# Attention weights and values of the two dilated groups stacked by residue

## The chip, the cores and the metric

The kernel runs on one core of a Trainium2 chip. The metric is the device time of one execution in microseconds (us); lower is better. The kernel before was timed three times: 780.74 us median, 780.69 to 781.08. One further execution was taken with the hardware profiler; it took 780.72 us, and its profile spans 778.9 us, so 1.82 us lie outside the span.

## The reference, cut to what matters

The model is a trunk of two layers on 256 tokens of width 1024. The first layer mixes tokens with a short convolution, the second with dilated window attention; each layer also has a squared-ReLU MLP (4096 wide) and a gated per-layer input. The change is inside the attention of the second layer. It has 8 heads of 128 channels, and each head exists in three groups with their own queries, keys and values:

```python
DILATED_PATTERNS = ((128, 1), (512, 4), (2048, 16))   # (window, dilation) of groups 0, 1, 2
...
    for g, (window, dilation) in enumerate(DILATED_PATTERNS):
        o_g, lse_g = dilated_window_attention(q[:, :, g], k[:, :, g], v[:, :, g], window, dilation)
        outs.append(o_g)
        lses.append(lse_g)
    weights = jax.nn.softmax(jnp.stack(lses, axis=0), axis=0)
    o = jnp.sum(weights[..., None] * jnp.stack(outs, axis=0), axis=0)
```

In group 0 a query sees the keys of up to 128 tokens back. In group 1 it sees only keys whose distance is a multiple of 4, in group 2 only keys whose distance is a multiple of 16. The three results are weighted by the softmax of their log-sums, which is the same as one softmax over the scores of all three groups side by side, followed by one sum over all their values.

## The kernel before, in words

**Number format.** Most products are done with each float32 operand split into two parts in the format `fp32r`: `hi`, the rounded value, and `lo`, the rest. ScalarE (ACT) writes `hi`, VectorE (DVE) writes `lo` by subtraction, and TensorE (PE) adds the products hi·hi, hi·lo and lo·hi in PSUM. Weights come from memory in slabs of up to 8 blocks of 128x128 (`load_to`, L335), are split by ACT (L356) and DVE (L295, the helper `sub`) in `split_to`, and used in `block` (L392). Five raw slabs and six split slabs are buffered, and `weights` asks for the split of the slab five ahead (`LOOK`, L34).

**Order.** `make_plan` (L139) writes the whole program out as one list: products, and steps (`("do", name, ...)`) between them. The scheduler of the tile language keeps this order as priority on every engine, and each engine then works through its own queue in order.

**Token order.** From the attention on, tokens are sorted by residue (`residue_order`, L41): first by t mod 4, then by t mod 16, then by t div 16. So each half `b` of 128 tokens holds two residues mod 4 of 64 tokens each. A query of groups 1 and 2 only ever sees keys of its own run of 64 tokens, since a distance that is a multiple of 4 keeps the residue mod 4. The kernel before uses only that it stays within its half of 128.

**One head**, with the lines the prediction speaks of:

- `qk` products give queries and keys, two banks of PSUM per group. `add_up` calls `sums` (L411 ACT, L412 DVE), which adds the two partial sums and frees the banks. `qk_out` (L639) applies the rotary embedding on GpSimd (POOL: L644, L647, L653), for head 0 in part on DVE. `qk_split` (L656) splits group 0 into hi and lo (L429 ACT, L295 DVE).
- `v` products give the values of all three groups, one bank per half of the tokens, 384 columns. `v_out` (L659) takes them out, scaled by the norm of each token: group 0 as hi (L665 ACT) and lo (L666 DVE), groups 1 and 2 together as 256 columns (L667 ACT) into `v12`, in plain float32.
- `scores` (L671): per half, three products of 256 columns for group 0 (L677) and one float32 product of 128 columns for each of groups 1 and 2 (L680), all into one bank of 512 columns. Then the softmax over 512 columns: mask and maximum (L683 DVE), the negated maximum (L686 DVE), exponential and sum (L687 ACT), reciprocal (L688 DVE), scaling (L689 ACT) in place into `sm`.
- `turn` (L692): four transposes of 128x128 per half (L698 PE), two for group 0 and one for each of groups 1 and 2, into two banks. The first is split into hi and lo (L429 ACT, L295 DVE), the second copied by ACT (L703) into `pT12`, 512 columns.
- `values` (L706): six products for group 0 (L713), then for each half and each of groups 1 and 2 one float32 product of 128 columns (L719), all added up in one bank. L730 (ACT) and L731 (DVE) split the result into hi and lo for the output product `w_o`.

A float32 product appears in the trace as two passes of PE, each with its own weight load (LDWEIGHTS, listed as engine PEld); an `fp32r` product and a transpose appear as one.

**Overlap.** While the products of head h run, the plan puts between them `scores`, `turn` and `values` of head h-1 (L198 to L205). For head 0 these steps come one place later (`late`), `values` of head 0 even within head 2. The steps of the last head lie between the `w_o` products (L208 to L213).

Of the kernel before, what the change touches and what calls it, by code (L numbers as in the profile page):

```python
# [12 lines left out]
AF = mybir.ActivationFunctionType  # L13
ALU = mybir.AluOpType

P = 128
S = 256
# [5 lines left out]
GROUPS = 3  # L23
# [17 lines left out]
def residue_order(t):  # L41

    return (t % 4) * 64 + (t % 16 // 4) * 16 + t // 16
# [210 lines left out]
def tile_trunk(ctx: ExitStack, tc: tile.TileContext, plan, slabs, ap, out):  # L254
    nc = tc.nc
# [10 lines left out]
    def act(name, dtype=F32):  # L266
        return apool.tile([P, 2, S], dtype, tag="act", name=name)
# [20 lines left out]
    def f32(t):  # L288
        return t.bitcast(F32)

    def flat(t):
        return t.rearrange("p i s -> p (i s)")
# [20 lines left out]
    rstd, rows, cur, mask, by_token = {}, {}, {}, {}, {}  # L313
# [5 lines left out]
    offsets, n = [], 0  # L319
# [6 lines left out]
    for si, s in enumerate(slabs):  # L326
# [3 lines left out]
        at = 0  # L330
# [71 lines left out]
    def close(name):  # L402
        opened.discard(name)

        return acc.pop(name)
# [21 lines left out]
    def split_into(kind, j, src):  # L427
        hi, lo, t = pair(f"{kind}{j}", "pp" if kind in ("p0", "p1") else "pair")
        nc.scalar.activation(hi, src, AF.Copy)  # L429
        sub(lo, src, hi)  # L430
        state[kind][j] = (hi, lo, t)
# [226 lines left out]

    def v_out(head):  # L659

        v0, v12 = act(f"v0_{head}", F32R), act(f"v12_{head}")
        for b in (0, 1):
            p, r = flat(close(("v", b, head))), rstd[3][:, b : b + 1]
            hi, lo = v0[:, b, :P], v0[:, b, P:]
            nc.scalar.activation(hi, p[:, :P], AF.Copy, scale=r)  # L665
            nc.vector.scalar_tensor_tensor(lo, p[:, :P], r, f32(hi), ALU.mult, ALU.subtract)  # L666
            nc.scalar.activation(v12[:, b, :], p[:, P : GROUPS * P], AF.Copy, scale=r)  # L667
        cur["v", head] = v0, v12


    def scores(head):  # L671
        for b in (0, 1):
            own = slice(b * P, (b + 1) * P)
            ps = psum.tile([P, 512], F32, tag="ps", name=f"sc{head}_{b}")
            hi, lo, _ = state["qk"][head]
            for n, (q, k) in enumerate(((hi, hi), (hi, lo), (lo, hi))):
                nc.tensor.matmul(ps[:, :S], q[:, 0, own], k[:, 1, :], start=n == 0, stop=n == 2)  # L677
            for g in (1, 2):
                t = cur["qk", head, g]
                nc.tensor.matmul(ps[:, (g + 1) * P : (g + 2) * P], t[:, 0, own], t[:, 1, own], start=True, stop=True)  # L680
# [7 lines left out]
            nc.vector.reciprocal(stats[2], stats[2])  # L688
            nc.scalar.activation(sm, sm, AF.Copy, scale=stats[2])  # L689
            cur["pr", head, b] = sm  # L690

    def turn(head):  # L692

        ps = [bank(f"tp{head}_{n}") for n in (0, 1)]
        for b in (0, 1):
            sm = cur.pop(("pr", head, b))
            for n in range(4):
                nc.tensor.transpose(  # L698
                    ps[n // 2][:, n % 2, b * P : (b + 1) * P], sm[:, n * P : (n + 1) * P], ident
                )  # L700
        split_into("pT", head, ps[0])
        t = act(f"pT12_{head}")
        nc.scalar.activation(t, ps[1], AF.Copy)  # L703
        cur["pT12", head] = t

    def values(head):  # L706
        ps = bank(f"o{head}")
        v0, v12 = cur.pop(("v", head))
        hi, lo, _ = state["pT"].pop(head)
        for kb in (0, 1):  # L710
            vhi, vlo = v0[:, kb, :P], v0[:, kb, P:]
            for n, (a, b) in enumerate(((vhi, hi), (vhi, lo), (vlo, hi))):
                nc.tensor.matmul(  # L713
                    ps[:, 0, :], a, b[:, kb, :], start=kb == 0 and n == 0, stop=False, skip_group_check=True
                )
        t = cur.pop(("pT12", head))
        for b in (0, 1):
            for g in (0, 1):
                nc.tensor.matmul(  # L719
                    ps[:, 0, b * P : (b + 1) * P],  # L720
                    v12[:, b, g * P : (g + 1) * P],
                    t[:, g, b * P : (b + 1) * P],
                    start=False,
                    stop=g == 1,
                    skip_group_check=True,
                )
# [3 lines left out]
        nc.scalar.activation(hi, ps[:, 0, :], AF.Copy)  # L730
        nc.vector.tensor_tensor(lo, ps[:, 0, :], f32(hi), ALU.subtract)  # L731
# [116 lines left out]
def masks():  # L848

    import numpy as np  # L850

    t = np.argsort([residue_order(t) for t in range(S)])
    m = np.full((P, 2, 512), NEG, np.float32)
    for b in range(2):
        q = t[b * P : (b + 1) * P, None]
        for keys, to, window, step in (
            (t, slice(0, S), 128, 1),
            (t[b * P : (b + 1) * P], slice(S, S + P), 512, 4),
            (t[b * P : (b + 1) * P], slice(S + P, S + 2 * P), 2048, 16),
        ):  # L860
            d = q - keys[None]
            m[:, b, to][(d >= 0) & (d <= window) & (d % step == 0)] = 0.0
    return m


# [56 lines left out]
```

## Time and profile before

| What | Before |
|---|---|
| median of 3 runs | 780.74 us |
| profiled execution, its span | 780.72 us, 778.9 us |
| PE busy | 770.7 us (99% of the span), 4860 matmuls |
| DVE, ACT, POOL busy | 570.9, 440.7, 166.8 us |
| granted TensorE clock | 0.998 |
| one middle head (437.97 to 467.06 us) | 29.09 us; PE 29.09, DVE 21.37, ACT 17.38, POOL 21.43 us busy |

Times in a trace are counted from the start of the span. In the view of single instructions a row gives the start, the length, the engine, the line, the operation, the tiles it writes and reads, how many instructions are merged, and in brackets how long the engine sat idle before it and for whom. A merged row reaches from the start of its first instruction to the end of its last. PE's rows overlap, since a product starts while the one before still drains; what a product costs in a dense stream is therefore the distance to the next one, not its own length. The chain of waits shows this distance directly: it gives, piece by piece, the time by which the end moved on.

### The profile page before, as it was taken

Reading aid. Unit: us, or ns where it says so; the run is one execution under the profiler, and the core shown is the slowest. Engines: PE = TensorE matmul, PEld = TensorE weight load, DVE = VectorE, ACT = ScalarE, POOL = GpSimd, SP = SyncE. Lnnn points to the kernel's source line nnn. Section 1 sums busy time; section 2 is a strip of 40 time slices with the busy share of each in tenths; the row PEclk is TensorE's granted clock in tenths of the full one; section 3 lists DMA queues with packets and bytes.
Section 4 is the critical chain, followed back from the end, with each engine's and each line's share of the span. In section 5 each row is a group of like instructions: output and inputs, shape, how many; then the busy total and the mean of one; then the engine's idle time right before and its main releaser. Section 6 shows DMA issues by size and latency. Waiting matters only on the chain.

```text
span 778.9 us, 12519 instructions
## 1 busy us (share of the span) xinstructions
PE 770.7 (99%) x4860; PEld 702.2 (90%) x4860; DVE 570.9 (73%) x817; ACT 440.7 (57%) x679; POOL 166.8 (21%) x110
## 2 busy tenths in 40 slices
PE   9999999999999999999999999999999999999996
PEld 8999998888888899989989989989988888888885
DVE  6897779898556669788768768767698887555564
ACT  8654565565444447557655655655675555444454
POOL 0000000000000000177867867865000000000002
PEclk9999999999999999999999999999999999999999
DMA  9855555655555554655455455455456555565521
GB/s 325 289 192 190 187 188 178 194 184 195 186 192 186 191 181 158 202 179 156 157 175 163 149 176 163 151 173 190 136 196 185 188 191 189 187 191 189 188 94 55
DMA packets 42539, 140.97 MB, mean 181 GB/s; under 512 B 4848, under 2 KB 6128, under 8 KB 42480
## 3 DMA queue, kind: packets, MB, share of 16 engines
q1 hardware_dynamic: 41904, 139.52, 56.1%
q8 instruction: 38, 0.62, 0.3%
q10 hardware_dynamic: 576, 0.66, 0.3%
q14 instruction: 21, 0.17, 0.1%
HBM read 139.10 MB, written 1.05 MB: 180 GB/s over the span
## 4 chain that ended last, share of the span: by engine, by line
PE 97%; issue 1%; DMA 1%; DVE 0%; POOL 0%; SPq 0%; POOLq 0%; ACT 0%; DVEq 0%
PE acc_u L392 23%; PE acc_d L392 23%; PE acc_qk L392 17%; PE acc_v L392 9%; PE acc_o L392 6%; PE acc_g L392 5%; PE acc_C L392 3%; PE acc_B L392 3%; PE acc_X L392 3%; PE acc_p L392 1%; PE o L719 1%; PE sc L680 1%; PE tp L698 1%; PE sc L677 1%; PE o L713 1%
## 5 line engine op out<-in xcount | busy, mean ns | idle before, releaser
L295 DVE TENSOR_TENSOR wlo<-raw,whi 128x1024 fp32r<-128x1024 f32 (+2 forms) x277 | 350.7, 1272 | 162.5 <-ACT whi L356 160.4
L356 ACT ACTIVATE whi<-raw 128x1024 fp32r<-128x1024 f32 (+2 forms) x277 | 278.2, 1007 | 220.6 <-PE acc_d L392 77.1
L392 PE MATMUL acc_d<-u,whi 128*128 128x512 f32 x512 | 160.8, 395 | 0.0
L392 PE MATMUL acc_u<-x,whi 128*128 128x512 f32 x512 | 160.8, 395 | 0.0
L392 PE MATMUL acc_qk<-x,whi 128*128 128x512 f32 (+1 forms) x432 | 134.5, 368 | 0.0
L392 PEld LDWEIGHTS acc_d<-u,wlo 128*128 128x128 f32 x512 | 96.2, 188 | 22.7
L392 PEld LDWEIGHTS acc_u<-x,wlo 128*128 128x128 f32 x512 | 96.2, 188 | 22.6
L462 POOL TENSOR_TENSOR n<-v,power 128x2 f32<-128x2 f32 (+1 forms) x6 | 3.9, 651 | 518.9 <-DVE v L487 514.4
L392 PE MATMUL acc_qk<-x,wlo 128*128 128x256 f32 x384 | 107.8, 281 | 0.0
L392 PE MATMUL acc_u<-x,wlo 128*128 128x256 f32 x512 | 101.2, 278 | 0.0
L392 PE MATMUL acc_d<-u,wlo 128*128 128x256 f32 x512 | 100.9, 278 | 0.0
L392 PEld LDWEIGHTS acc_qk<-x,whi 128*128 128x128 f32 x432 | 77.9, 188 | 13.7
L647 POOL TENSOR_TENSOR rot<-qk,sinr 16x512 f32<-16x512 f32 x44 | 78.3, 1780 | 3.0
L392 PEld LDWEIGHTS acc_d<-u,whi 128*128 128x128 f32 x512 | 78.0, 189 | 0.0
L392 PEld LDWEIGHTS acc_u<-x,whi 128*128 128x128 f32 x512 | 77.9, 189 | 0.0
L392 PEld LDWEIGHTS acc_qk<-x,wlo 128*128 128x128 f32 x384 | 72.5, 189 | 0.0
L392 PE MATMUL acc_v<-whi,x 128*128 128x384 f32 x256 | 68.9, 339 | 0.0
L644 POOL TENSOR_TENSOR qk<-qk,cosr 128x512 f32<-128x512 f32 x22 | 36.8, 1671 | 53.7 <-DVE qk L412 41.9
L392 PEld LDWEIGHTS acc_v<-whi,x 128*128 128x128 f32 x256 | 46.6, 188 | 0.0
L392 PE MATMUL acc_o<-y,whi 128*128 128x256 f32 x256 | 46.4, 283 | 0.0
L653 POOL TENSOR_TENSOR qk<-qk,rot 48x512 f32<-48x512 f32 x22 | 42.9, 1950 | 1.7
L392 PE MATMUL acc_v<-wlo,x 128*128 128x384 f32 x128 | 42.8, 335 | 0.0
(169 smaller groups left out, 1036.2 us busy)
## 6 DMA issues: line engine op xcount, KB each, us to landing
raw<-in_w SPq DMA_DIRECT2D x230, 512.0 KB, 3.4
raw<-in_w SPq DMA_DIRECT2D x32, 384.0 KB, 3.1
raw<-in_w SPq DMA_DIRECT2D x10, 256.0 KB, 4.8
h<-in_xT SPq DMA_DIRECT2D x4, 256.0 KB, 5.1
mask<-in_mask SPq DMA_DIRECT2D x2, 256.0 KB, 4.1
gain<-in_gain SPq DMA_DIRECT2D x2, 256.0 KB, 4.9
out<-htg SPq DMA_DIRECT2D x2, 256.0 KB, 2.1
raw<-in_w ACTq DMA_DIRECT2D x2, 128.0 KB, 3.4
```

The source lines that it names most:

```text
L295: nc.vector.tensor_tensor(out, a, f32(b), ALU.subtract)
L356: nc.scalar.activation(hi[:, :width], t[:, :width], AF.Copy)
L392: nc.tensor.matmul(to, a, b, start=n == 0 and name not in opened, stop=n == len(products) - 1 and left[name, half if kind == "n" else 0] == 0,
L462: nc.gpsimd.tensor_tensor(y, v, power[:, : v.shape[1]], ALU.pow)
L644: engine.tensor_tensor(t, p, both(cosr), ALU.mult)
L647: engine.tensor_tensor(r[dst : dst + 16], p[src : src + 16], sinr[src : src + 16].unsqueeze(1).to_broadcast([16, 2, S]), ALU.mult,)
L653: engine.tensor_tensor(t[:48], t[:48], r[:48], ALU.add)
L677: nc.tensor.matmul(ps[:, :S], q[:, 0, own], k[:, 1, :], start=n == 0, stop=n == 2)
L680: nc.tensor.matmul(ps[:, (g + 1) * P : (g + 2) * P], t[:, 0, own], t[:, 1, own], start=True, stop=True)
L698: nc.tensor.transpose(ps[n // 2][:, n % 2, b * P : (b + 1) * P], sm[:, n * P : (n + 1) * P], ident)
L713: nc.tensor.matmul(ps[:, 0, :], a, b[:, kb, :], start=kb == 0 and n == 0, stop=False, skip_group_check=True)
L719: nc.tensor.matmul(ps[:, 0, b * P : (b + 1) * P], v12[:, b, g * P : (g + 1) * P], t[:, g, b * P : (b + 1) * P], start=False, stop=g == 1, ...
```

## The change: what it does

The tokens' runs of 64 are used. For a query in the first run of its half (r = 0), only the first 64 keys of the half count in groups 1 and 2; for r = 1, only the second 64. So the 2 x 128 score columns of groups 1 and 2 are laid out as four pieces of 64: (group 1, first run), (group 2, first run), (group 2, second run), (group 1, second run). A query of run r needs only 128 of these 256 columns: those of its own run, with both groups side by side.

- `scores`: the product of group 1 writes its 128 columns as two pieces of 64 with a gap of 128 columns between them; group 2 writes the middle 128. The mask in memory has the same new layout and the same size. The softmax still runs over 512 columns. The scaling goes into a new tile `pr` and is three instructions per half in place of one: 256 columns for group 0 on all 128 partitions, and for each run 128 columns on 64 partitions.
- `turn`: three transposes per half in place of four; the third holds groups 1 and 2 of each query's own run. `pT12` and its copy are 256 columns in place of 512.
- `v_out`: the values of groups 1 and 2 are stacked to match, 64 partitions of one group above 64 of the other. Per half that is four copies of 128 columns on 64 partitions, two of them to other partitions than they come from, in place of one copy of 256 columns on 128 partitions.
- `values`: still four float32 products per head, now one per run, with 64 columns in place of 128, each summing over both groups.

```diff
     def v_out(head):
...
-            nc.scalar.activation(v12[:, b, :], p[:, P : GROUPS * P], AF.Copy, scale=r)
+            for r in (0, 1):
+                own, other = (slice(n * 64, (n + 1) * 64) for n in (r, 1 - r))
+                for g, to in ((1, own), (2, other)):
+                    nc.scalar.activation(
+                        v12[to, b, r * P : (r + 1) * P], p[own, g * P : (g + 1) * P], AF.Copy, scale=scale[own]
+                    )
...
     def scores(head):
...
-                nc.tensor.matmul(ps[:, (g + 1) * P : (g + 2) * P], t[:, 0, own], t[:, 1, own], start=True, stop=True)
+                out = ps[:, S + (g - 1) * 64 :]
+                out = out[:, :P] if g == 2 else out.rearrange("p (n c) -> p n c", c=64)[:, 0:4:3, :]
+                keys = t[:, 1, own] if g == 2 else t[:, 1, own].rearrange("p (n c) -> p n c", c=64)
+                nc.tensor.matmul(out, t[:, 0, own], keys, start=True, stop=True)
...
-            nc.scalar.activation(sm, sm, AF.Copy, scale=stats[2])
-            cur["pr", head, b] = sm
+            pr = flat(act(f"pr{head}_{b}"))
+            nc.scalar.activation(pr[:, :S], sm[:, :S], AF.Copy, scale=stats[2])
+            for r in (0, 1):
+                q = slice(r * 64, (r + 1) * 64)
+                nc.scalar.activation(
+                    pr[q, S : S + P], sm[q, S + r * P : S + (r + 1) * P], AF.Copy, scale=stats[2][q]
+                )
+            cur["pr", head, b] = pr
...
     def turn(head):
...
-            for n in range(4):
+            for n in range(3):
                 nc.tensor.transpose(
                     ps[n // 2][:, n % 2, b * P : (b + 1) * P], sm[:, n * P : (n + 1) * P], ident
                 )
         split_into("pT", head, ps[0])
-        t = act(f"pT12_{head}")
-        nc.scalar.activation(t, ps[1], AF.Copy)
-        cur["pT12", head] = t
+        t = cur["pT12", head] = act(f"pT12_{head}")[:, 0, :]
+        nc.scalar.activation(t, ps[1][:, 0, :], AF.Copy)
...
     def values(head):
...
-        for b in (0, 1):
-            for g in (0, 1):
-                nc.tensor.matmul(
-                    ps[:, 0, b * P : (b + 1) * P],
-                    v12[:, b, g * P : (g + 1) * P],
-                    t[:, g, b * P : (b + 1) * P],
-                    start=False,
-                    stop=g == 1,
-                    skip_group_check=True,
-                )
+        for n in range(4):
+            q, r = slice(n * 64, (n + 1) * 64), n % 2
+            nc.tensor.matmul(
+                ps[:, 0, q],
+                v12[:, n // 2, r * P : (r + 1) * P],
+                t[:, q],
+                start=False,
+                stop=n == 3,
+                skip_group_check=True,
+            )
```

More of the change, by code (lines that the diff above doesn't have):

```diff
@@ L855, in masks @@
         q = t[b * P : (b + 1) * P, None]
[L856 to L859, printed above, removed]
+        half = t[b * P : (b + 1) * P]
+        first, second = half[:64], half[64:]
+        for keys, at, window, step in (
+            (t, 0, 128, 1),
+            (first, S, 512, 4),
+            (first, S + 64, 2048, 16),
+            (second, S + 128, 2048, 16),
+            (second, S + 192, 512, 4),
         ):
             d = q - keys[None]
-            m[:, b, to][(d >= 0) & (d <= window) & (d % step == 0)] = 0.0
+            m[:, b, at : at + len(keys)][(d >= 0) & (d <= window) & (d % step == 0)] = 0.0
     return m
```

6 lines of the change are left out of this document (3 added, 3 removed).

## The prediction

> **What bounds the kernel now.** I read the engines' shares on the page first, then the chain of waits, then one middle head as a stretch of its own (its columns: length, then PE, weight loads, DVE, ACT and POOL busy, the granted clock).
>
> ```profile
> PE 770.7 (99%) x4860; PEld 702.2 (90%) x4860; DVE 570.9 (73%) x817; ACT 440.7 (57%) x679; POOL 166.8 (21%) x110
> ```
>
> ```profile
> PE 97%; issue 1%; DMA 1%; DVE 0%; POOL 0%; SPq 0%; POOLq 0%; ACT 0%; DVEq 0%
> ```
>
> ```profile
> 437.97:467.06 29.09, 29.09 (x182) 27.03 (x181) 21.37 (x30) 17.38 (x30) 21.43 (x13) 1.00 0.54 167
> ```
>
> The chain is PE for 97%, and in a middle head PE has no gap: 29.09 of 29.09 us. Time is won only by taking distance out of PE's stream, and lost only where PE has to wait. ACT, DVE and POOL each have 7 to 12 us free in a head. The chain inside that head gives each piece's share of PE's time:
>
> ```profile
> 438.25 0.87 PE tp L698 x8
> 439.13 6.27 PE acc_v L392 x36
> 445.40 0.71 PE o L713 x6
> 446.11 0.89 PE o L719 x8
> 447.00 2.08 PE acc_v L392 x12
> 449.08 5.55 PE acc_qk L392 x32
> 454.63 0.35 PE sc L677 x3
> 454.99 0.44 PE sc L680 x4
> ```
>
> Eight transposes move the end on by 0.87 us, 0.109 each. Eight passes of L719 take 0.89, 0.111 each; four of L680 take 0.44, 0.110 each. A pass of 384 columns (acc_v) takes 6.27/36 = 0.174, that is 0.45 ns a column, by which 128 columns would need 0.058. Something other than columns paces the small passes, at about 0.11.
>
> **The change part by part.** *Transposes.* Two fewer a head, 16 in all: 16 x 0.109 = **-1.74 us**, straight out of PE's stream. The passes of L680 stay as they are in number.
>
> *Products of 64 columns.* L719 keeps its 64 passes; only the columns streamed are halved. The nearest narrower row is the sum for the norm (L477, 2 columns), by its weight loads (PEld) beside those of L719, and in the chain:
>
> ```profile
> L477 PE MATMUL ssq<-ones,tot x16: 165/251/251, 29.8 to 754.1; 128*128 128x2 f32 x16
> ```
>
> ```profile
> 29.68 0.54 PEld L477 LDWEIGHTS ssq<-ones,tot 128*128 128x128 f32 x4
> 30.14 0.19 PEld L392 LDWEIGHTS acc_C<-x,wlo 128*128 128x128 f32 x1
> ```
>
> ```profile
> 445.83 0.98 PEld L719 LDWEIGHTS o<-pT,v 128*128 128x128 f32 x8
> 446.73 0.19 PEld L392 LDWEIGHTS acc_v<-whi,x 128*128 128x128 f32 x1
> ```
>
> ```profile
> 29.97 0.34 PE ssq L477 x4
> ```
>
> With 2 columns a load follows every (30.14 - 29.68)/4 = 0.115 us, with 128 columns every (446.73 - 445.83)/8 = 0.113. The load of the 128x128 weights is the pace, and the change leaves its size alone. The chain shows 0.34 for four passes of 2 columns, 0.10 less than for four of L680; that is the shorter drain of the last one, and I expect the next piece to give it back, as it starts by its loads. Bounds: 0, or 0.10 a head, 0.8 us in all. I take 0, because the loads, which go on into the next piece, show no gain. The Trainium skill weighs in on both sides (TensorE: Matmul & The Clock Gate): under "LDWEIGHTS (loading the stationary operand)" a load takes its number of columns over 1.2, an estimate of 107 ns here, whatever streams, with which the rows agree; under "Back-to-back issue gap" an isolated gap is the streamed columns over 2.4 plus 2.5 ns, by which 64 columns in place of 128 would save 27 ns on each of 64 passes, another 1.7 us. The rows speak for the first.
>
> *The split destination of group 1's score product.* No row shows a PE output in two pieces. The nearest rows are two DVE additions of 256 columns, one through a regrouped order and one straight:
>
> ```profile
> L635 DVE TENSOR_TENSOR hr<-h,gs 128x256 f32<-128x256 f32 x8 | 4.7, 630 | 0.1
> L449 DVE TENSOR_TENSOR tot<-sq 128x256 f32<-128x256 f32 x24 | 10.1, 419 | 0.0
> ```
>
> There the order costs a factor 1.5. On PE the stream of 128 columns (0.058) has 0.053 of cover under the load of 0.111, so up to a factor 1.9 is hidden. Bounds: 0, or passes twice as long, 32 x 0.111 = +3.55 us; I take 0, as one break in 128 columns is far from that regrouping.
>
> No step is moved in the plan, no queue is passed, and no DMA is added: the mask keeps its size.
>
> *More work on ACT.* Its rows:
>
> ```profile
> L667 ACT ACTIVATE v<-acc_v,n 128x256 f32<-128x256 f32 x16 | 6.7, 470 | 3.5 <-DVE v L666 3.5
> L665 ACT ACTIVATE v<-acc_v,n 128x128 fp32r<-128x128 f32 x16 | 5.8, 368 | 8.6 <-PE acc_v L392 8.6
> L689 ACT ACTIVATE sm<-sm,st 128x512 f32<-128x512 f32 x16 | 10.6, 710 | 0.8 <-DVE st L688 0.8
> L438 ACT ACTIVATE x<-h,gains 128x256 fp32r<-128x256 f32 x24 | 10.9, 502 | 1.3 <-DVE h L618 1.0 <-DMA h<-in_xT 0.2
> L703 ACT ACTIVATE pT<-tp 128x512 f32<-128x512 f32 x8 | 4.7, 588 | 0.0
> L730 ACT ACTIVATE y<-o 128x256 fp32r<-128x256 f32 x8 | 3.1, 384 | 4.6 <-PE o L719 4.6
> ```
>
> Eight copies like L665 in place of two like L667: +8 x 0.368 - 2 x 0.470 = +2.00 us a head (half the partitions should not be faster or slower). Scaling: 256 columns as in L438, 0.502, and on the line from 710 (512) to 502 (256) some 0.398 for 128: 2 x (0.502 + 2 x 0.398 - 0.710) = +1.18. The shorter copy of `pT12` gives back 0.588 - 0.384 = 0.20. Together +2.98 on 17.38 of 29.09: ACT does not become the bound. What matters is who waits.
>
> The weight splits do not: ACT waits for PE to free split buffers, not the reverse (28.0 us in 18 waits on the products of queries and keys alone). Five slabs of 8 blocks of 2 x 5.55/32 us are 13.9 us of lead, less about 2.4 for the split itself.
>
> ```profile
> ACT whi L356 <- PE acc_qk L392: 28.0, 18, 2.5
> ```
>
> Nor do PSUM's banks. In a middle head the copies of the values end at 450.34 + 0.83 = 451.17, later by 1.2 us (eight at a distance of 0.25, as two like L665 take 0.61 in a row, in place of 0.84), and only then are the two banks of `v` free. The scores ask for theirs after 454; until then `v`, the values' sum and the next queries and keys hold five of the eight.
>
> ```profile
> 450.34 0.83 ACT L667 ACTIVATE v<-acc_v,n 128x256 f32<-128x256 f32 x2
> ```
>
> ```profile
> 360.71 0.61 ACT L665 ACTIVATE v<-acc_v,n 128x128 fp32r<-128x128 f32 x2
> ```
>
> The softmax in a middle head ends its scaling at 430.21 + 1.32 = 431.53, and the transposes come after 438; in the last head at 550.56 against 552.14.
>
> ```profile
> 430.21 1.32 ACT L689 ACTIVATE sm<-sm,st 128x512 f32<-128x512 f32 x2
> ```
>
> ```profile
> 549.24 1.32 ACT L689 ACTIVATE sm<-sm,st 128x512 f32<-128x512 f32 x2
> ```
>
> ```profile
> 552.14 1.03 PE L698 MATMUL tp<-ident,sm 128*128 128x128 f32 x8
> ```
>
> In a row two such instructions follow each other faster than they last (1.32, not 1.42), so I expect +0.8 for the scaling, with the bounds 0.6 and 1.2. That fits under 6.6 and under 1.58. **Head 0 has no such cover:**
>
> ```profile
> 338.25 0.84 ACT L667 ACTIVATE v<-acc_v,n 128x256 f32<-128x256 f32 x2 [1.83 <-DVE v L666]
> 338.98 0.39 ACT L411 ACTIVATE qk<-acc_qk 128x256 f32<-128x256 f32 x1
> 339.25 0.64 ACT L429 ACTIVATE qk<-qk 128x512 fp32r<-128x512 f32 x1
> 339.77 0.39 ACT L411 ACTIVATE qk<-acc_qk 128x256 f32<-128x256 f32 x1
> ```
>
> ```profile
> 350.23 0.63 ACT L429 ACTIVATE qk<-qk 128x512 fp32r<-128x512 f32 x1 [0.74 <-POOL qk L653]
> ```
>
> ```profile
> 355.67 1.34 ACT L689 ACTIVATE sm<-sm,st 128x512 f32<-128x512 f32 x2 [0.75 <-DVE st L688]
> ```
>
> ```profile
> 338.40 2.07 DVE L295 TENSOR_TENSOR wlo<-raw,whi 128x1024 fp32r<-128x1024 f32 x2
> ```
>
> ```profile
> 341.22 3.42 POOL L644 TENSOR_TENSOR qk<-qk,cosr 128x512 f32<-128x512 f32 x1 [5.36 <-DVE qk L412]
> ```
>
> ```profile
> 357.12 1.03 PE L698 MATMUL tp<-ident,sm 128*128 128x128 f32 x8
> ```
>
> Scaling ends at 357.01, the transposes start at 357.12. After the change the sixth and last is due at 357.12 + 5 x 0.109 = 357.67, and its columns are the last to be scaled: 357.01 + 0.8 = 357.81, and the weight load has to follow. In front of that stands a longer way. The copies of `v_out` wait for DVE's L666 (1.83) and hold up ACT's queue; eight in place of two push the L411 behind them by the same 1.2. DVE's L412, then POOL's rotary step (341.22) of head 1 come later by up to 0.7, since DVE was busy with two splits until 340.47 anyway; ACT's L429 waits for POOL (0.74), and behind it in ACT's queue stands the softmax of head 0. So PE waits 0.1 to 1.0 us here, once; 0 if the scheduler lays ACT's queue out otherwise. I take **+0.5**, the middle.
>
> *Sum:* -1.74 + 0.5 = -1.24 us. On the profiled execution's 780.72 that is 779.48; it lies 0.02 below the median, so 779.5.
>
> **The rivals.** *No wait in head 0* (ACT's queue in another order, or POOL faster when DVE is idle): the whole 1.74, 779.0. For it: in the middle head shown PE never waited, and a scheduler that lets ready work go first can put the softmax ahead of L429. Against it: 357.01 beside 357.12.
>
> *The narrow products are faster too.* If columns paced them, 64 x 0.055 = 3.55 more, 775.4. Against it stands 0.115 with 2 columns.
>
> *The split destination slows PE.* One mechanism, on PE's path in every head: at twice the distance -1.74 + 3.55 = +1.8, 782.5; slower than before from 1.74/32 = 54 ns a pass on, which is the cover computed above used up and as much again. The Trainium skill (PSUM — Partial Sum Buffer, "Specifications (TRN2)") says that non-contiguous access slows matmuls significantly; no run so far shows it. By that sentence this rival would be the likely one; the rows give the pace to the weight load, so I leave it small.
>
> *A longer tail of waits*: POOL, not ACT alone, falls behind in head 1, whose scores need its last group, and PE waits 1.5 to 2.5 in all: 780.5 to 781.5.
>
> **How the numbers follow.** Chances: forecast 0.50 (its own range 779.1 to 779.9), no wait 0.30, narrow products 0.05, split destination 0.08, longer waits 0.07. The predicted time is the forecast's, 779.5. The range 778.7 to 780.9 takes in the forecast, the full gain and the lower half of the longer waits, about 0.83. A measurement of this kernel tells about 0.2%, 1.56 us, from no change, so faster means below 779.18. That holds no wait, narrow products and the lowest tenth of the forecast: 0.40. Slower, above 782.3, are the split destination and what of the waits goes beyond 1.5 us more than I give them: 0.10. The rest, 0.50, is the same.
>
> **What would show it.** Transposes 48, six in 0.65 in the chain; L719's successor still at 0.11 a pass; L680's too, with a split destination or without; 64 copies at L667's place near 0.37; the scaling pair of head 0 ending after 357.5 and a gap of PE before its last transposes, with middle heads 0.22 shorter (28.87) and free of gaps. A middle head of 29.09 or more, or a narrow pass at 0.06, would prove me wrong.

## The result and the profile after

The changed kernel takes 786.26 us (median of 4 runs, 786.06 to 786.50), the kernel before beside it 780.81 (4 runs, 780.69 to 781.08): a ratio of 1.0070 with a 95% interval of 1.0058 to 1.0082. It is slower by 5.45 us. The forecast was 779.5, the range ended at 780.9. The profiled execution spans 784.3 us in place of 778.9.

The engines' shares and the chain of waits on the page of the kernel after:

```profile
PE 770.2 (98%) x4844; PEld 699.9 (89%) x4844; DVE 587.6 (75%) x817; ACT 464.1 (59%) x759; POOL 165.6 (21%) x110
...
PE 89%; DVE 4%; ACT 3%; issue 3%; DMA 1%; POOL 0%; SPq 0%; POOLq 0%; DVEq 0%; ACTq 0%
```

The 16 transposes are gone from the count. The chain, 97% PE before, now passes through DVE, ACT and issue times for 10% of the span: PE waits somewhere. It is not in the middle heads. One of them as a stretch (the columns are those of the stretch in the prediction) and its chain:

```profile
459.56:488.41 28.85, 28.85 (x181) 26.79 (x180) 23.56 (x29) 19.31 (x40) 21.34 (x12) 1.00 0.50 153
```

```profile
470.67 0.66 PE tp L715 x6
471.33 6.24 PE acc_v L392 x36
477.57 0.71 PE o L729 x6
478.28 0.84 PE o L735 x8
479.12 2.14 PE acc_v L392 x12
481.26 5.55 PE acc_qk L392 x32
486.81 0.35 PE sc L684 x3
487.16 0.44 PE sc L690 x4
```

This head is what was forecast: PE is busy for all of 28.85 us (before: 29.09), six transposes in 0.66, four passes with the split destination in 0.44 as before. The narrow products take 0.84 in place of 0.89, but the piece behind them takes 2.14 in place of 2.08: 2.98 against 2.97, nothing won.

To find the loss I cut the chain at four places that both kernels have: the first query and key products of the attention, the 32 behind the transposes of head 0, the first `w_o` products and the first MLP products of the layer. First the kernel before, then the kernel after:

```profile
306.26 13.68 PE acc_qk L392 x114
...
360.24 5.55 PE acc_qk L392 x32
...
536.31 8.63 PE acc_o L392 x72
...
563.61 22.30 PE acc_u L392 x128
```

```profile
306.57 13.68 PE acc_qk L392 x114
...
364.28 5.55 PE acc_qk L392 x32
...
540.16 7.28 PE acc_o L392 x61
...
568.90 22.37 PE acc_u L392 x128
```

| Stretch | Before | After | Change |
|---|---|---|---|
| start to the first products | 306.26 | 306.57 | +0.31 |
| first stretch (head 0 and its transposes) | 53.98 | 57.71 | +3.73 |
| middle stretch (to the first `w_o` products) | 176.07 | 175.88 | -0.19 |
| last stretch (last head, `w_o`) | 27.30 | 28.74 | +1.44 |

Together +5.29; the first 0.31 lies in front of the attention and inside what the versions below show for this stretch (306.25 to 306.68). The saving is about 0.23 a head (29.09 to 28.85), so six heads would make the middle stretch 174.67, as versions below show; the kernel after loses 1.2 there, 1.75 in the last stretch (26.99 below) and 3.9 in head 0. The view of waits names the place:

```profile
PE tp L715 <- ACT pr L701: 4.0, 3, 1.5
PEld o L729 <- DVE pT L295: 1.2, 2, 0.9
```

L715 are the transposes, L701 the scaling of group 0's columns. They wait three times, twice in head 0 and once in the last head. The single instructions in head 0, the transposes of the first and of the second half of the tokens:

```profile
358.98 0.44 PE L715 MATMUL tp<-ident,pr 128*128 128x128 f32 x2 [1.38 <-ACT pr L701]
...
363.08 0.44 PE L715 MATMUL tp<-ident,pr 128*128 128x128 f32 x2 [1.48 <-ACT pr L701]
```

**Why the softmax of head 0 is late.** Back along its inputs: ACT's copies of the values, POOL's rotary step of head 1, and the two maxima (DVE). Rows of the kernel after, and of the first maximum before:

```profile
338.54 3.00 ACT L671 ACTIVATE v<-acc_v,n 64x128 f32<-64x128 f32 x8 [1.80 <-DVE v L667]
```

```profile
342.82 1.30 POOL L644 TENSOR_TENSOR qk<-qk,cosr 128x512 f32<-128x512 f32 x1 [6.67 <-DVE qk L412]
...
344.20 3.58 POOL L647 TENSOR_TENSOR rot<-qk,sinr 16x512 f32<-16x512 f32 x2
```

```profile
351.92 0.68 DVE L683 CUSTOM_DVE_ANT_0 sm<-sc,mask 128x512 f32<-128x512 f32 x1
```

```profile
L693 DVE CUSTOM_DVE_ANT_0 sm<-sc,mask x2: 665/672/678, 355.6 to 358.0; 128x512 f32<-128x512 f32 x2
```

The eight copies take 3.00 us in a row, 0.84 before. Everything behind them on ACT moves: POOL starts at 342.82 in place of 341.22. And the maxima come at 355.6 and 358.0: the first 3.7 late (0.3 of it is the later start of this execution), more than the copies explain, the second 2.3 behind it where it stood 0.6 behind. Two more things happen in between.

DVE's weight splits in this stretch, before and then after (shortest, median and longest in ns, then the first and last start):

```profile
L295 DVE TENSOR_TENSOR wlo<-raw,whi x5: 943/944/1772, 339.5 to 347.8; 128x768 fp32r<-128x768 f32 x4, 128x1024 fp32r<-128x1024 f32 x1
```

```profile
L295 DVE TENSOR_TENSOR wlo<-raw,whi x4: 2037/2168/2628, 344.6 to 351.7; 128x768 fp32r<-128x768 f32 x3, 128x1024 fp32r<-128x1024 f32 x1
```

The same subtraction of 128x768 takes 0.94 us in three of four cases before (1.77 in the one that starts at 345.0) and 2.0 to 2.6 after. Before, two of them run beside POOL's L644, which is then the slow one (3.42 us, quoted in the prediction); after, L644 takes 1.30 and the splits, from 344.6 on, stand beside POOL's L647 instead. In all 14 profiles this goes with which engine comes first at L644 (341.22 before, 342.82 after). DVE's split of the queries and keys, before and then after:

```profile
341.07 0.67 DVE L295 TENSOR_TENSOR qk<-qk,qk 128x512 fp32r<-128x512 f32 x1
```

```profile
342.92 1.75 DVE L295 TENSOR_TENSOR qk<-qk,qk 128x512 fp32r<-128x512 f32 x1 [0.18 <-ACT qk L429]
```

Before, it starts 0.15 us ahead of L644; after, it waits for ACT's L429 and starts 0.10 behind. From DVE's L412 in front of it (340.40 before, 341.99 after) to the first maximum the same instructions then take 13.7 us in place of 11.5. DVE had 3.2 us free between 341 and 352 before; the slower instructions eat them, and the rest pushes the maximum.

The second thing is the order: the maximum of the second half now stands behind the scaling of the first half in every head. The experiments separate the two.

### The profile page after: what moved, and what is told of

Same layout as the page of the kernel before. It is cut to its first block, busy times and chain, and to the rows that moved or that the text cites. A ratio compares the mean times of both kernels' runs of the same rounds, so it can differ in the third digit from the quotient of the medians.

```text
span 784.3 us, 12587 instructions
## 1 busy us (share of the span) xinstructions
PE 770.2 (98%) x4844; PEld 699.9 (89%) x4844; DVE 587.6 (75%) x817; ACT 464.1 (59%) x759; POOL 165.6 (21%) x110
## 4 chain that ended last, share of the span: by engine, by line
PE 89%; DVE 4%; ACT 3%; issue 3%; DMA 1%; POOL 0%; SPq 0%; POOLq 0%; DVEq 0%; ACTq 0%
PE acc_u L392 23%; PE acc_d L392 23%; PE acc_qk L392 14%; PE acc_v L392 6%; PE acc_g L392 5%; PE acc_o L392 5%; PE acc_C L392 3%; PE acc_B L392 3%; PE acc_X L392 3%; DVE wlo L295 2%; PE acc_p L392 1%; PE o L735 1%; ACT whi L356 1%; PE o L729 1%; PE sc L690 1%
## 5 line engine op out<-in xcount | busy, mean ns | idle before, releaser
L295 DVE TENSOR_TENSOR wlo<-raw,whi 128x1024 fp32r<-128x1024 f32 (+2 forms) x277 | 366.5, 1332 | 145.8 <-ACT whi L356 143.3
L392 PEld LDWEIGHTS acc_qk<-x,whi 128*128 128x128 f32 x432 | 77.9, 188 | 13.7
L647 POOL TENSOR_TENSOR rot<-qk,sinr 16x512 f32<-16x512 f32 x44 | 83.1, 1889 | 3.0
L644 POOL TENSOR_TENSOR qk<-qk,cosr 128x512 f32<-128x512 f32 x22 | 31.6, 1437 | 62.3 <-DVE qk L412 47.4
```

The costliest lines, as they stand in the source:

```text
L295: nc.vector.tensor_tensor(out, a, f32(b), ALU.subtract)
L392: nc.tensor.matmul(to, a, b, start=n == 0 and name not in opened, stop=n == len(products) - 1 and left[name, half if kind == "n" else 0] == 0,
L644: engine.tensor_tensor(t, p, both(cosr), ALU.mult)
L647: engine.tensor_tensor(r[dst : dst + 16], p[src : src + 16], sinr[src : src + 16].unsqueeze(1).to_broadcast([16, 2, S]), ALU.mult,)
```

## The experiments

Theories on trial. **Copies** (B in the expectations): the eight copies of 64 partitions are too long, and DVE beside POOL makes more of it. **Tile** (A): the new tile `pr` makes the two halves of a softmax run one after the other. From the second round on, C says that the copies cost only where a step of the plan has too little cover, D that ACT and DVE are too full with any such copies. Against both: the narrow products or the split destination slow PE (the middle head already speaks against it), or there is simply no room at head 0 and a wait that is removed comes back elsewhere. In the comparisons the kernel before is at 780.9, 780.7 and 780.7 us. Columns of the summary at the end of this section are the three stretches of the table above.

**1. `inplace`: no new tile.**

```diff
-            pr = flat(act(f"pr{head}_{b}"))
+            pr = sm
```

> The changed kernel with the scaling written back in place into sm instead of into a tile of its own (pr); all else as changed. Theory A (the new tile takes its buffer from the same pool as sm, buffers are handed out in the order of the program, so the second half's maximum cannot be queued before the first half's scaling; both halves of the softmax run one after the other): the two maxima stand next to each other again, the wait of 1.8 us in the last head and that before the second half's transposes in head 0 (1.6 us) go, 782 to 783 us. Theory B (only ACT's eight copies of the values matter): the order of the maxima has no weight, 785.5 to 786.5.

Measured 782.77 us, ratio 1.0026 (1.0017 to 1.0035). The halves stand together again, still late:

```profile
L693 DVE CUSTOM_DVE_ANT_0 sm<-sc,mask x2: 679/680/682, 355.4 to 356.0; 128x512 f32<-128x512 f32 x2
```

The middle and last stretches become 174.67 and 26.99, so no wait is left there. Head 0 keeps 57.02. That is theory A's forecast: one line is worth 3.5 us, most of it outside head 0.

**2. `one_copy`: the new tile, but the two copies of before.**

```diff
-            for r in (0, 1):
...
-                        v12[to, b, r * P : (r + 1) * P], p[own, g * P : (g + 1) * P], AF.Copy, scale=scale[own]
-                    )
+            nc.scalar.activation(v12[:, b, :], p[:, P : GROUPS * P], AF.Copy, scale=scale)
```

> The changed kernel with the values of groups 1 and 2 taken out by one copy of 128x256 per half as before, not stacked, so groups 1 and 2 are summed with the wrong values; this leaves out the stacking alone. Theory A (the halves of the softmax run one after the other because of the tile pr): the waits in head 0 and the last head stay for the most part, 784 to 786. Theory B (eight copies at 0.375 us without overlap, 3.0 us in place of 0.84, hold up the queues): head 0's first wait and the waits of the values in heads 6 and 7 (1.2 us) go, 782 to 783.

Measured 779.64, ratio 0.9984 (0.9975 to 0.9993). First stretch 54.39, middle 174.67. The halves are still one after the other (351.9 and 354.3), yet it hardly costs. Both theories had expected 782 or more.

**3. `inplace_one_copy`: both edits.**

> Both: scaling in place and one copy of the values per half, not stacked (groups 1 and 2 get the wrong values). Theories A and B together leave nothing but PE's saving: 779.0, middle heads 28.84 us, no wait of PE in attention. If the split destination or the narrow products cost something of their own, it stays above 780.

Measured 779.47, ratio 0.9983 (0.9974 to 0.9992): the forecast's 779.5, in a kernel without the stacking. It is 0.5 above what was expected of this run; by the view of waits 0.3 of it is a wait left at head 0's transposes.

**4. `before_tile`: the kernel before with the scaled weights in a new tile.**

```diff
-            nc.scalar.activation(sm, sm, AF.Copy, scale=stats[2])
-            cur["pr", head, b] = sm
+            pr = flat(act(f"pr{head}_{b}"))
+            nc.scalar.activation(pr, sm, AF.Copy, scale=stats[2])
+            cur["pr", head, b] = pr
```

> The kernel before, with the scaled softmax written into a new tile of the same pool instead of in place, nothing else. Theory A: the maximum of the second half moves behind the reciprocal of the first in the scheduled order, the last head's cover of 1.58 us is overrun and PE waits there and in head 0; 782 to 784. Theory B: no change, 780.5 to 781.1.

Measured 781.65, ratio 1.0009 (1.0000 to 1.0017), with the order of the kernel after:

```profile
L683 DVE CUSTOM_DVE_ANT_0 sm<-sc,mask x2: 673/676/680, 352.0 to 354.4; 128x512 f32<-128x512 f32 x2
```

So the tile alone makes the order. The time lies between the two forecasts: 0.7 us are lost, 0.5 of them in head 0, and the wait expected in the last head does not come (last stretch 27.43). The four versions around the change:

| us | `sm` scaled in place | new tile `pr` |
|---|---|---|
| two copies of 128x256 | 779.47 | 779.64 |
| eight copies of 64x128 | 782.77 | 786.26 |

The copies cost 3.3 alone, the tile 0.2 alone, and 6.8 together. They don't add up, which fits that each uses the slack that the other needs. The waits of head 6 and of the last head appear only with both, but for 0.2 us in `one_copy`.

**5. `before_eight` and 6. `before_eight_wide`: the kernel before with eight copies, by partitions or by columns.** Nothing is stacked; the same data goes to the same place.

```diff
-            nc.scalar.activation(v12[:, b, :], p[:, P : GROUPS * P], AF.Copy, scale=r)
+            for q in (slice(0, 64), slice(64, P)):
+                for g in (1, 2):
+                    nc.scalar.activation(
+                        v12[q, b, (g - 1) * P : g * P], p[q, g * P : (g + 1) * P], AF.Copy, scale=r[q]
+                    )
```

```diff
+            for n in range(4):
+                at = slice(n * 64, (n + 1) * 64)
+                nc.scalar.activation(v12[:, b, at], p[:, P + n * 64 : P + (n + 1) * 64], AF.Copy, scale=r)
```

> The kernel before with the values of groups 1 and 2 taken out by eight copies of 64 partitions x 128 columns in place of two of 128x256, each to the place where it was, nothing else. Theory B (the copies alone make head 0's transposes late): eight copies take 3.0 us in a row, the maximum of head 0 moves from 352 to 355, PE waits 2.5 to 3.5 us there, 783 to 784.5. Theory A (only together with the serial halves of the softmax): 780.7 to 781.3.

> The kernel before with eight copies of 128 partitions x 64 columns instead. If copies on half of the partitions cannot overlap each other and those on all partitions can, eight follow each other at about 0.2 us, 1.6 to 1.8 us in all in place of 3.0, and PE waits less in head 0: 781 to 782. If it is the number of instructions that counts and not their partitions, they follow each other at 0.3 us without overlap, 2.5 us, and the time is near that of the 64-partition copies.

Measured 782.53, ratio 1.0022 (1.0013 to 1.0032), and 780.84, ratio 1.0002 (0.9993 to 1.0011). The copies of the first, then of the second:

```profile
338.65 2.50 ACT L669 ACTIVATE v<-acc_v,n 64x128 f32<-64x128 f32 x8 [1.80 <-DVE v L666]
```

```profile
338.38 1.75 ACT L669 ACTIVATE v<-acc_v,n 128x64 f32<-128x64 f32 x8 [1.80 <-DVE v L666]
...
351.69 0.68 DVE L685 CUSTOM_DVE_ANT_0 sm<-sc,mask 128x512 f32<-128x512 f32 x1
```

Copies on 64 partitions cost by themselves, if less than theory B's 783 to 784.5; the number of instructions is not what costs: eight in 1.75 us are free, eight in 2.50 cost 1.8 us, with the maximum at 355.3. What DVE does behind them decides. Its busy time from 341 to 352 us (third number in us behind the length), before, `before_eight_wide` and after:

```profile
341.00:352.00 11.00, 11.00 (x70) 9.95 (x69) 7.80 (x11) 5.53 (x9) 10.48 (x6) 1.00 0.84 270
```

```profile
341.00:352.00 11.00, 11.00 (x70) 9.92 (x69) 10.82 (x11) 6.91 (x12) 10.35 (x6) 1.00 0.78 245
```

```profile
341.00:352.00 11.00, 11.00 (x70) 9.91 (x69) 9.84 (x9) 8.20 (x16) 8.89 (x6) 1.00 0.57 189
```

In the wide version DVE is slowed by POOL as well (10.82 of 11 busy), but its L412 begins at 340.5 as before, its split comes ahead of L644, and the first maximum follows 11.2 us behind L412. After, L412 begins at 342.0 and the maximum follows 13.7 behind. No profile here lies in between: 11.2 to 11.6 us where the split comes ahead of L644, 13.7 where it comes behind, also in `inplace_three` below, whose L412 is only 0.6 late.

**7. `before_shift` and 8. `inplace_shift`: more room for head 0.** `turn` of head 0 moves half a group later, into the first group's products of head 2, and `values` of head 0 into the second group's.

```diff
-        plan += qk(h, 0, range(NK)) + ([("do", "values", 0)] if h == 2 else []) + sums(h, 0)
+        if h == 2:
+            plan += qk(h, 0, range(4)) + [("do", "turn", 0)] + qk(h, 0, range(4, NK)) + sums(h, 0)
...
+        if h == 2:
+            plan += qk(h, 1, range(4)) + [("do", "values", 0)] + qk(h, 1, range(4, NK)) + sums(h, 1)
```

> The kernel before with the same move of head 0's transposes and values, nothing else. Both theories: PE had no wait there, so no change, 780.6 to 781.2; if it were faster by itself, the gain of the run beside it would not be the stacking's.

> The changed kernel with the scaling in place, and with the plan's steps of head 0 moved: its transposes stand after half of head 2's first group of queries and keys (4.85 us later), its values after half of the second group. Theory C (the eight copies cost nothing on PE but where a step of the plan has too little cover; after the scaling in place that is the transposes of head 0 alone, which wait 3.2 us): the wait goes and PE's saving of 1.74 us shows, 779.0 to 779.5. Theory D (ACT and DVE are too full with the eight copies, so a step that is moved away only hands the wait on to the next, the values of head 0 or the scores of head 1): 781 to 783.

Measured 780.75, ratio 1.0000 (0.9992 to 1.0009): the move itself costs nothing. With the change 782.09, ratio 1.0021 (1.0012 to 1.0030), where `inplace` had 1.0026. The wait at the transposes is gone, and another has come, of query and key products of head 2, which the view of waits puts down to the next copies of the values (L678 here):

```profile
PE acc_qk L399 <- ACT v L678: 2.1, 2, 1.2
```

Moving the transposes hands the wait on, as theory D had it.

**9. `inplace_three`: half the copies.** The score columns lie in the order group 1, group 2, group 1, group 2, so that both products have a split destination and one wide copy brings half of the values to their place; two copies across partitions remain per half.

```diff
+            nc.scalar.activation(v12[:, b, :], p[:, P : GROUPS * P], AF.Copy, scale=scale)
+            for to, at, src, g in ((slice(64, P), 0, slice(0, 64), 2), (slice(0, 64), 1, slice(64, P), 1)):
+                nc.scalar.activation(
+                    v12[to, b, at * P : (at + 1) * P], p[src, g * P : (g + 1) * P], AF.Copy, scale=scale[src]
+                )
...
-                out = ps[:, S + (g - 1) * 64 :]
+                out = ps[:, S:].rearrange("p (n c) -> p n c", c=64)[:, g - 1 : 4 : 2, :]
```

> The changed kernel with the scaling in place and the stacking by three copies a half in place of four: one of 128x256 for everything, then two of 64x128 over it for the pieces that go to other partitions (the pieces of the second run stand in the order group 1, group 2, so both score products write two pieces). ACT's six copies should take about 2.2 us in a row in place of 3.0. Theory C (what counts is how late ACT's copies make head 0's softmax): between the in-place kernel (782.8) and the one with a single copy (779.5), 780.5 to 782. Theory D (any second form of copying leaves DVE and ACT too full): 782 to 783.

Measured 782.92, ratio 1.0023 (1.0012 to 1.0034). The copies still take 2.3 us (0.84 + 1.49), and the maximum is at 354.7, 0.7 earlier than in `inplace`. A second thing keeps the first stretch at 57.85. The stretch with the waits, the one behind it and the next (the number before the last two is the granted clock):

```profile
357.00:360.20 3.20, 1.49 (x8) 0.56 (x7) 0.80 (x3) 3.05 (x9) 3.06 (x3) 0.98 0.42 123
360.30:363.30 3.00, 3.00 (x10) 3.00 (x11) 2.06 (x2) 3.00 (x5) 2.92 (x2) 0.50 0.00 0
363.30:366.30 3.00, 3.00 (x18) 2.74 (x18) 3.00 (x3) 2.13 (x4) 0.30 (x1) 0.97 0.68 155
```

PE runs at half its clock for about 3 us after having waited, worth about 1.5 us. This parts the executions of three versions by their mean granted clock:

| us | at 0.995 | at 0.997 or more |
|---|---|---|
| `inplace` | 783.44 to 783.87 (4) | 782.10 to 783.13 (6) |
| `inplace_shift` | 782.82 to 783.41 (5) | 781.37 to 782.09 (6) |
| `inplace_three` | 782.50 to 783.11 (5) | 781.31, 781.47 (2) |

So the medians hide a gain. At the higher clock half the copies win about 0.8 us over `inplace`, inside theory C's 780.5 to 782, and the move of experiment 8 about 0.6. The profiles of these two were taken at 0.995.

**10. `inplace_dma`: the stacking by DMA.** ACT copies the values as before; four transfers a head on SP's queue stack them.

```diff
+            nc.scalar.activation(v12[:, b, :], p[:, P : GROUPS * P], AF.Copy, scale=scale)
+        natural, v12 = v12, act(f"vs{head}")
+        low, high = slice(0, 64), slice(64, P)
+        for to, r, src, g in ((low, 0, low, 0), (high, 0, low, 1), (low, 1, high, 0), (high, 1, high, 1)):
+            nc.sync.dma_start(v12[to, :, r * P : (r + 1) * P], natural[src, :, g * P : (g + 1) * P])
```

> The changed kernel with the scaling in place, one copy of 128x256 a half on ACT as before the change, and the stacking by four DMAs a head from one tile to another (64 partitions each, both halves of the tokens). Theory C: ACT's queue is as short as with a single copy, the values are needed only 15 us later, so 779.3 to 780.0 with the right result. Theory D: 781 or more.

Measured **779.64, ratio 0.9986 (0.9977 to 0.9995)**: this version does the whole change and beats both kernels, by 1.1 us against before. Its transfers (KB each, median us to landing) and its chain at the transposes of two neighbouring heads:

```profile
vs<-v SPq DMA_DIRECT2D x32, 64.0 KB, 2.1
```

```profile
438.44 0.66 PE tp L713 x6
...
467.29 0.66 PE tp L713 x6
```

The heads are 28.85 apart. First stretch 54.44, middle 174.67, last 26.99. Some 0.7 of wait remains in head 0. This is theory C's forecast.

**11. `narrow_three` and 12. `narrow_dma`: only the scores that count.** One product of 64 rows and 64 columns per run and group, and the softmax over 384 columns in place of 512, so the scaling is one instruction again; the copies as in 9 and the DMAs as in 10.

```diff
+                for r in (0, 1):
+                    run = slice(b * P + r * 64, b * P + (r + 1) * 64)
+                    out = ps[r * 64 : (r + 1) * 64, S + (g - 1) * 64 : S + g * 64]
+                    nc.tensor.matmul(out, t[:, 0, run], t[:, 1, run], start=True, stop=True, skip_group_check=True)
```

> As the kernel with three copies, but the score products of groups 1 and 2 are made per run of 64 queries and 64 keys (four products of 64x64 a half in place of two of 128x128), so that the stacked scores are 128 columns from the start: maximum, exponential and scaling run over 384 columns in place of 512, each in one instruction. DVE and ACT lose about 0.13 us an instruction, the scaling is one again. Theory C: the softmax of head 0 is ready 1 us or more earlier, 779.5 to 780.5 if a weight load of 64 columns takes half as long as one of 128; if it takes as long, PE has 8 more passes of 0.11 a head, 7 us in all, 786 to 788.

> The same narrow scores with the stacking by DMA and one copy a half on ACT. ACT and DVE do less than in the kernel before. Theory C: no wait of PE in attention, 779.0 to 779.5 with weight loads of 64 columns at half the time, 786 to 788 with loads at the full time.

Measured 782.05, ratio 1.0017 (1.0008 to 1.0026), and 781.17, ratio 1.0006 (0.9997 to 1.0015). Both lie outside all that was expected. The first has the wait of head 0 (0.6 by the view of waits, first stretch 54.97), the second has none there: its first stretch is 54.01. But its middle stretch is 176.39, 1.7 more than with `inplace_dma`. The scores in its chain:

```profile
455.39 0.38 PE sc L689 x8
455.77 0.55 PE sc L683 x3
...
456.70 11.30 PE acc_qk L392 x64
```

Eight passes of 64 columns of weights take 0.38, less than four of 128 (0.44); the pieces behind them take 0.55 and 11.30 where they took 0.36 and 11.11. What the shorter loads win is lost again, and more, in the pieces behind them, and that eats the saving of the transposes.

| us | Time | First | Middle | Last |
|---|---|---|---|---|
| before | 780.8 | 53.98 | 176.07 | 27.30 |
| after | 786.3 | 57.71 | 175.88 | 28.74 |
| `inplace` | 782.8 | 57.02 | 174.67 | 26.99 |
| `one_copy` | 779.6 | 54.39 | 174.67 | 27.16 |
| `inplace_one_copy` | 779.5 | 54.31 | 174.68 | 27.00 |
| `before_tile` | 781.7 | 54.49 | 176.22 | 27.43 |
| `before_eight` | 782.5 | 55.73 | 176.08 | 27.28 |
| `before_eight_wide` | 780.8 | 54.01 | 176.07 | 27.30 |
| `inplace_three` | 782.9 | 57.85 | 174.69 | 27.00 |
| `inplace_dma` | 779.6 | 54.44 | 174.67 | 26.99 |
| `narrow_three` | 782.1 | 54.97 | 176.39 | 27.12 |
| `narrow_dma` | 781.2 | 54.01 | 176.39 | 27.13 |

Times are medians, stretches those of the profiled execution. The two shifted versions have no cut at the same place.

## Why the prediction was wrong

**What held.** The transposes: 0.66 for six, and a head 0.23 to 0.24 shorter, a little more than 0.22. The products of 64 columns at nothing: the row of 2 columns told it rightly. The split destination at nothing: 0.44 for four passes, and in `inplace_three`, with both products split, the middle stretch is 174.69. Under "Specifications (TRN2)" the page PSUM — Partial Sum Buffer of the Trainium skill says that non-contiguous access slows matmuls significantly; two runs of 64 columns under a weight load don't show it. The scaling: where it stands in a row, in head 0 of `inplace`, it takes 2.45 us in place of 1.34, +1.1, inside the bounds of 0.6 and 1.2. ACT did not become the bound in the middle heads. The place was right too: head 0. Neither of the two signs that the prediction named as proof against it (a middle head of 29.09 or more, a narrow pass at 0.06) came, and it was wrong all the same.

**Where it failed, in order.** The term that failed is the +0.5 for PE's wait: head 0 lost 3.9, and head 6 and the last head, which the sum put at nothing, 1.2 and 1.75.

1. *"Eight at a distance of 0.25, as two like L665 take 0.61 in a row."* The copies lie 0.375 apart (3.00/8) and don't overlap at all; I took the distance from rows of 128 partitions and wrote that half the partitions should make no difference. In a row they take 2.16 us more than the two before, not 1.2 (and a distance of 0.25 would have given 1.28). The Trainium skill (ScalarE: Activation LUTs, "What ACT_TABLE_LOAD costs") lets instructions in a row overlap by 93 ns; copies by columns on all partitions do better than that here (0.33 us long, 0.20 apart, eight in 1.75), those on 64 partitions don't (0.36 long and 0.31 apart in their place, 0.375 apart where half of them change partitions).

2. *"POOL's rotary step … later by up to 0.7"*, and from there a wait of +0.5. POOL started 1.6 later (1.3 without the later start of this execution), but the real error is that I shifted the rows behind it with their lengths unchanged. DVE and POOL slow each other, and a shift changes which one pays. DVE's lengths were taken from a schedule that no longer held; the way to the maximum grew from 11.5 to 13.7 us, and the maximum came 3.7 late. The Trainium skill has the rule (SBUF — State Buffer, "Who interferes with whom"): a DVE instruction with two inputs from SBUF and a POOL instruction that reads it exclude each other, and the order in which they are issued decides who waits. The traces agree in kind: where DVE's split starts 0.15 us ahead of L644, in the kernel before, POOL is the slow one (3.42 against 1.30); where it starts 0.10 behind, after, DVE is (1.75 against 0.67), and again beside L647 (2.0 to 2.6 against 0.94). In `before_eight_wide`, 0.12 ahead, both pay (L644 1.73, the next split 1.94). The prediction's row of L644 at 3.42 us, where the next L644 of the same trace takes 1.28, was a sign of it.

3. *"No step is moved in the plan, no queue is passed."* In the plan none is, but the new tile changed the order all the same: `before_tile` shows it with nothing else changed. The reason I hold likely, from the code, is that `pr` shares its buffers' tag with `sm`, and buffers of one tag are handed out in program order, so the second half's tile is asked for behind the first half's `pr`; a tag of its own was not run. With two copies it costs 0.2 in the changed kernel and 0.7 in the kernel before, with eight 3.5.

4. *"That fits under 6.6 and under 1.58."* The first held. In the last head the second half's scaling ended at 558.30 and the transposes waited for it, since its maximum stood behind the first half's scaling; `inplace` has no wait there. The rows of the last head after:

```profile
551.22 0.69 DVE L693 CUSTOM_DVE_ANT_0 sm<-sc,mask 128x512 f32<-128x512 f32 x1
...
554.07 0.67 DVE L693 CUSTOM_DVE_ANT_0 sm<-sc,mask 128x512 f32<-128x512 f32 x1
...
557.50 0.80 ACT L704 ACTIVATE pr<-sm,st 64x128 f32<-64x128 f32 x2
```

5. *"The weight splits do not [wait]"* spoke of the splits, not of what stands behind them. In head 6 the small split of `pT` stood behind three weight splits of 2.09 each, again beside POOL, and the products of the values waited:

```profile
529.40 6.27 DVE L295 TENSOR_TENSOR wlo<-raw,whi 128x768 fp32r<-128x768 f32 x3 [0.39 <-ACT whi L356]
...
535.59 0.68 DVE L295 TENSOR_TENSOR pT<-tp,pT 128x512 fp32r<-128x512 f32 x1
```

`inplace` has no wait there. The chain of the kernel after reaches these splits through both halves of head 6's softmax, which take 7.3 us from the first maximum to the end of the last scaling (520.50 to 527.81), where `inplace` needs 6.3 (516.95 to 523.28). Where the rest of the delay comes from is open.

The rival of a longer tail of waits, by POOL falling behind in head 1, was the nearest; it spoke of POOL being late, not of DVE's rows growing longer. It got 0.07 and 1.5 to 2.5 us; about 6.9 were lost (3.9 + 1.2 + 1.75).

## What to carry to other kernels

Where a step on a side engine gets longer, don't only shift what stands behind it: where DVE and POOL run side by side, look at which of their rows are longer than their shortest, and ask who will stand beside whom after the shift. The cost need not grow with the shift: copies of 1.75 us in place of 0.84 cost nothing here, and with copies of 2.3 us another engine came first, which made the way to the maximum 2.2 us longer at one stroke; copies of 3.0 us made it no longer than that. A new tile in place of an update in place can change the order of other work; and a rearrangement across partitions may be cheaper on an idle DMA queue than on a busy engine.

## What the runs showed of the hardware

- **ACT on 64 partitions.** Eight copies of 64x128: 3.00 us where four of them go to other partitions, 2.50 where all stay in their place. Eight of 128x64, half as many columns and the same data: 1.75. The two scalings of 64x128 take 0.80. Halving the partitions saves nothing (0.36 us each; 0.37 for 128x128 in L665) and costs most of the overlap (0.31 to 0.375 apart; 0.24 in the pair of L665).
- **DVE beside POOL.** The split of 128x768 takes 0.94 us beside L644 in the kernel before, and 1.8 to 2.6 beside POOL's 16x512 steps, though these touch 16 partitions only. A change of 0.25 us in who comes first (0.15 ahead, 0.10 behind) goes with 2.2 us on DVE.
- **The clock after a wait.** In `inplace_three` the granted clock fell to 0.50 for about 3 us after PE had waited. In the kernel after, with longer waits, it stayed at 1.00 (rows below). The Trainium skill (TensorE: Matmul & The Clock Gate, "What's actually happening") tells of a window of some 3.4 us that runs freely, and of half clock after an idle one. The length fits, but PE was not idle for a window here: it was busy for 1.49 of the 3.20 us before. How much waiting brings the half clock is open. In `inplace`, `inplace_shift` and `inplace_three` the executions at a mean clock of 0.995 are 1.5 us slower in the median than those at 0.997 or more, which is what the half clock costs in the profile of `inplace_three`.

Two stretches of the kernel after, in and between its waits:

```profile
357.00:360.00 3.00, 1.35 (x8) 0.80 (x7) 3.00 (x5) 2.96 (x7) 2.92 (x2) 1.00 0.32 82
360.00:363.00 3.00, 1.59 (x10) 1.27 (x8) 2.50 (x5) 2.85 (x6) 2.94 (x2) 1.00 0.57 183
```

- **Shorter weight loads.** Loads of 64 columns are faster (0.38 for eight against 0.44 for four of 128), but the pieces behind them get longer by as much and more (0.19 each at two places shown).
